# Input and modulation weights laid out in 4 KB runs, small vectors merged, and one engine's order written out in the first stage of a two-layer attention and convolution backbone

## The chip, the cores and the metric

The kernel runs on one core of a Trainium2 chip. The metric is device microseconds of one execution, the median of three runs. A profiled execution of the same kernel gives the trace: the span from its first to its last instruction, and the engines PE (matrix products), DVE (vector), ACT (scalar and activation), POOL (general) and SP, whose queue issues nearly all DMA transfers. "PEld" is PE's loading of weights, and a "q" behind an engine's name marks its queue issuing a DMA.

## The reference, cut to what matters

```
# latent x: 1024 tokens of 1024 channels, context ctx: 256 tokens, conditioning vectors c and c_ctx; all float32
# layer 0 is windowed attention, layer 1 a Conformer convolution
shift, scale, gate     = split(silu(c)    @ ada_w[0] + ada_b[0], 3)
shift_c, scale_c, ...  = split(silu(c_ctx) @ ada_w[0] + ada_b[0], 3)
h_lat = rmsnorm(x, norm_g[0])   * (1 + scale)   + shift
h_ctx = rmsnorm(ctx, norm_g[0]) * (1 + scale_c) + shift_c
proj  = h_lat @ attn_w_in        # 16 query heads, 4 key and 4 value heads, 16 gate heads, 128 columns each
...                              # windowed softmax with a sink and all context keys, times silu(z), @ attn_w_out
x     = x + gate * y
...                              # layer 1: modulation by ada_w[1], ada_b[1]; @ conv_w_in + conv_b_in; GLU; depthwise
...                              # convolution of 31 taps; LayerNorm; silu; times silu(z); @ conv_w_out; x + gate * y
out   = rmsnorm(x, final_g)
```

## The kernel before

Every float32 product is made of three fp32r products: a matrix is split into a rounded part (`hh`, `whi`) and a remainder (`hl`, `wlo`), and `mm3` issues three matmuls of 128x512. A weight column block is 1024x128. `WStream` loads one ("wraw", 512 KB), ACT copies it to `whi`, DVE or POOL subtracts to `wlo`.

The data lives in 45 pages of 128x1024 float32, handed out in the order in which they came free. A DMA into a page waits until the page's last reader is done, and everything behind it in SP's queue waits too. A scheduler orders the instructions of each engine, except of engines named in `pin(...)`: those keep the order of the program.

The first stage computes the modulation and the first three column blocks (k, q and v of the first head). It works on eight channel tiles `kt` of 128 channels. For each tile:

- `ada_load(kt)` has loaded 1 MB of `ada_w`: the shift and scale columns of this tile, in two pages `araw`.
- `ada_mm(kt)` multiplies them with silu(c) and silu(c_ctx) (`c32`): sixteen small matmuls. They leave four partial sums, at partitions 0, 32, 64 and 96, which DVE adds to a row tile `R` ("arow"). Partition 4 of it holds `ada_b`, and the other partitions are zeroed ahead by POOL.
- `ada_cols(kt)` multiplies the rows by a 0/1 matrix `sel`, which adds the parts and turns them into columns; DVE writes them into `mods[kt]` ("mod").
- `turn(xs0, kt)` transposes four 128x128 pieces of the normalised first 512 tokens into `psg`.
- `x_tile` makes `hh` (ACT), `hf` (DVE) and `hl` (DVE) of it, and `x_mm` adds the tile's three matmuls to each of three accumulators in `pss`.

Around it stand `sums` (the squares of a row tile on ACT, into "junk", with their sum in "ssx"), `rstd_of` and `scale_rows`, which normalise the rows ("x_page<-x_page,r"). They run for the first 512 tokens `xs0` at the start, for the second 512, `xs1`, while the tiles go by, and for the context `cx` at the end. `spin` issues matmuls on zeros at the very start. After the eight tiles the second 512 tokens follow in the same manner (`turn(xs1, ...)`, `x_tile(..., half 1)`), then the context; then head by head the rest of the projection and the attention, with four more `wraw` loads issued at once between the two. The convolution layer and the final normalisation end the program.

Of the kernel before, what the change touches and what calls it, by code (L numbers as in the profile page):

```python
# [14 lines left out]
P = 128  # L15
# [79 lines left out]
def backbone_kernel(  # L95
    ctx_stack: ExitStack,
    tc: tile.TileContext,
    x, c, ctx, c_ctx, ada_w, ada_b, norm_g, attn_w_in, attn_sink, attn_w_out,
    conv_w_in, conv_b_in, conv_dw_w, conv_dw_b, conv_ln_g, conv_ln_b, conv_w_out, final_g,
    k_cos, k_sin, k_mask, k_ident, k_sel,  # L100
# [61 lines left out]
    ident = ctile([P, P], F32, "ident")  # L162
    vt = ctile([P, P], F32, "vt")
    sel = vt[:, 112:114]
    sink = ctile([P, 2 * NH], F32, "sink")[:, 0:NH]
# [7 lines left out]
    crow = crow_pg[0:32, 0:P]  # L173
# [28 lines left out]
    class WStream:  # L202
# [52 lines left out]
    W = attn_w_in[0]  # L255

    def wcol(c0):
        return W[:, c0:c0 + P]
# [39 lines left out]

    def load_vecs():
        v = pg.alloc(F32, [2 * P], "vecs")  # L300
# [1430 lines left out]
```

## Time and profile before

| | |
|---|---|
| median of three runs | 1729.6 us (1728.45 to 1730.24) |
| the profiled execution's own time | 1727.67 us |
| its span | 1725.9 us, 24046 instructions |
| granted TensorE clock over the span | 0.993 |
| busy share of the span | PE 98%, PEld 83%, DVE 64%, POOL 52%, ACT 51% |
| moved by DMA | 242.46 MB in 203533 packets; 134999 of them under 2 KB |

A row of the timeline reads: start and duration in microseconds, engine, line, operation, the tiles written and read (out<-in), shape, how many instructions were merged, and in brackets how long the engine stood idle before it and who ended that. Almost all rows have line 89, a helper that records every operation, so the tiles tell the place. A row of the windows reads: the stretch, its length, the busy time of PE, PEld, DVE, ACT and POOL with instruction counts, the granted clock, the DMA share and GB/s.

### The profile page before, as it was taken

The numbers are of one execution on the slowest core, as the hardware profiler recorded it, in microseconds if no ns is written. First come the engines' busy times: TensorE is split into PE (matmuls) and PEld (weight loads), VectorE is DVE, ScalarE is ACT, GpSimd is POOL, SyncE is SP. The second block draws the span as 40 slices with busy tenths as digits, with TensorE's granted clock in tenths as the row PEclk, the third lists the DMA queues.
The fourth block names the chain that finished last, engine by engine and source line by source line (L and its number), as shares of the span: only waits on it lengthen the run. The fifth ranks groups of instructions, "written<-read, shape, count | busy, mean of one in ns | idle before, by whom it ended". The sixth has DMA issues, their size and how long they took to land.

```text
span 1725.9 us, 24046 instructions
## 1 busy us (share of the span) xinstructions
PE 1694.5 (98%) x8489; PEld 1425.7 (83%) x8489; DVE 1096.1 (64%) x2090; ACT 873.3 (51%) x1531; POOL 895.4 (52%) x741
## 2 busy tenths in 40 slices
PE   8799999999999999999999999999999999999997
PEld 5588888888888888888888888888888888788886
DVE  4655553555445553555315179999999999967923
ACT  3555553555345444545334355564665565466731
POOL 1145664566636565653101257999998888130400
PEclk9899999999999999999999999999999999999999
DMA  9334443444334543436777723011121202376971
GB/s 284 124 101 142 136 137 84 147 150 149 99 107 147 159 141 88 135 121 205 252 262 245 258 86 110 25 49 37 42 82 38 91 32 80 122 251 246 337 270 49
DMA packets 203533, 242.46 MB, mean 140 GB/s; under 512 B 11807, under 2 KB 134999, under 8 KB 203413
## 3 DMA queue, kind: packets, MB, share of 16 engines
q1 hardware_dynamic: 197012, 230.43, 40.4%
q10 hardware_dynamic: 6400, 10.49, 2.5%
q8 instruction: 67, 1.10, 0.3%
q14 instruction: 54, 0.43, 0.1%
HBM read 188.70 MB, written 41.69 MB: 133 GB/s over the span
## 4 chain that ended last, share of the span: by engine, by line
PE 91%; DMA 3%; DVE 2%; SPq 2%; ACT 1%; issue 1%; POOL 1%; ACTq 0%; DVEq 0%; POOLq 0%
PE psg L89 47%; PE pss L89 23%; PE pso L89 20%; SPq L89 2%; DMA low_page<-in_conv_w_out_dram 1%; DMA rope_half<-rope_half 1%; DMA x_page<-in_x_dram 0%; DMA araw_page<-in_ada_w_dram 0%; POOL rope_half L89 0%; DVE hf_page L89 0%; DMA ozf_page<-ozd 0%; DMA wraw_page<-in_attn_w_in_dram 0%; ACT lhi_half L89 0%; DVE hl_page L89 0%; DVE ptlo L89 0%
## 5 line engine op out<-in xcount | busy, mean ns | idle before, releaser
L89 POOL TENSOR_TENSOR odd_half<-odd_half,prod_half 128x513 f32<-128x513 f32 (+2 forms) x252 | 313.5, 1251 | 23.3 <-ACT prod_half L89 10.0
L89 PE MATMUL psg<-hh_page,whi_page 128*128 128x512 f32 x600 | 235.6, 393 | 0.0
L89 PE MATMUL psg<-hl_page,whi_page 128*128 128x512 f32 x600 | 234.4, 391 | 0.0
L89 PE MATMUL psg<-hh_page,wlo_page 128*128 128x512 f32 x600 | 233.9, 390 | 0.0
L89 POOL TENSOR_TENSOR wlo_page<-wraw_page,whi_page 128x512 fp32r<-128x512 f32 (+1 forms) x106 | 177.5, 1690 | 96.4 <-ACT whi_page L89 71.1
L89 ACT ACTIVATE prod_half<-ubuf,dww 128x513 f32<-128x513 f32 (+2 forms) x252 | 165.4, 675 | 115.0 <-POOL odd_half L89 111.3
L89 POOL TENSOR_SCALAR p_page<-p_page,sc 128x640 f32<-128x640 f32 (+1 forms) x128 | 99.1, 774 | 223.9 <-DVE sc L89 218.1
L89 PE MATMUL psg<-h2h_page,whi_page 128*128 128x512 f32 x464 | 181.9, 392 | 0.0
L89 PE MATMUL psg<-h2h_page,wlo_page 128*128 128x512 f32 x464 | 180.6, 389 | 0.0
L89 PE MATMUL psg<-h2l_page,whi_page 128*128 128x512 f32 x464 | 180.6, 389 | 0.0
L89 DVE SCALAR_TENSOR_TENSOR pss<-ubuf,dww,pss 128x512 f32<-128x512 f32 (+3 forms) x270 | 172.7, 672 | 0.1
L89 DVE SCALAR_TENSOR_TENSOR pss<-ubuf,wsum,pss 128x512 f32<-128x512 f32 (+3 forms) x270 | 172.0, 672 | 0.2
L89 DVE TENSOR_TENSOR ptlo<-pss,pthi 128x640 fp32r<-128x640 f32 (+1 forms) x144 | 103.5, 719 | 85.7 <-ACT pthi L89 84.6
L89 ACT ACTIVATE pthi<-pss 128x640 fp32r<-128x640 f32 (+1 forms) x144 | 88.7, 616 | 107.9 <-PE pss L89 98.1
L89 ACT ACTIVATE p_page<-p_page,sc 128x641 f32<-128x641 f32 (+1 forms) x128 | 102.6, 802 | 75.0 <-DVE sc L89 71.3
L89 PEld LDWEIGHTS psg<-hh_page,wlo_page 128*128 128x128 f32 x600 | 112.7, 188 | 24.4
L89 PEld LDWEIGHTS psg<-hh_page,whi_page 128*128 128x128 f32 x600 | 112.8, 188 | 19.4
L89 PEld LDWEIGHTS psg<-hl_page,whi_page 128*128 128x128 f32 x600 | 112.8, 188 | 18.4
L89 ACT ACTIVATE whi_page<-wraw_page 128x1024 fp32r<-128x1024 f32 x88 | 92.6, 1052 | 60.0 <-PE psg L89 19.7
L89 PE MATMUL pso<-h2h_page,whi_page 128*128 128x512 f32 x304 | 118.3, 389 | 0.0
L89 PE MATMUL pso<-h2l_page,whi_page 128*128 128x512 f32 x304 | 118.3, 389 | 0.0
L89 PE MATMUL pso<-h2h_page,wlo_page 128*128 128x512 f32 x304 | 118.3, 389 | 0.0
(247 smaller groups left out, 4019.5 us busy)
## 6 DMA issues: line engine op xcount, KB each, us to landing
wraw_page<-in_conv_w_in_dram SPq DMA_DIRECT2D x48, 512.0 KB
wraw_page<-in_attn_w_in_dram SPq DMA_DIRECT2D x40, 512.0 KB
wol_page<-wolA SPq DMA_DIRECT2D x32, 512.0 KB
wo_page<-in_attn_w_out_dram SPq DMA_DIRECT2D x32, 512.0 KB
wo_page<-in_conv_w_out_dram SPq DMA_DIRECT2D x32, 512.0 KB
wol_page<-wolC SPq DMA_DIRECT2D x32, 512.0 KB
rope_half<-rope_half ACTq DMA_DIRECT2D x80, 128.0 KB
araw_page<-in_ada_w_dram SPq DMA_DIRECT2D x32, 256.0 KB
```

The costliest lines, as they stand in the source:

```text
L89: r = f(*a, **k)
```

## The change

The host hands the weights over in another layout: each 1024x128 column block of `attn_w_in` and `conv_w_in`, and each half tile of the modulation weight of layer 0, is one contiguous block in which a partition's 1024 values stand in one run of 4 KB. Before, such a load read runs of 512 bytes. Each `araw` page is now one DMA instead of two.

The small vectors come in two loads: `k_rows` (c, c_ctx, norm_g and the shift and scale part of `ada_b[0]`, 48 rows) at the start, and `k_vecs` (128 rows), now behind the loads of `xs1` and `cx`. The 0/1 matrix `sel` rides in the load of the identity. The `ada_b` part no longer stands in the row tile: it is transposed with c at the start into columns `bcol` (the scale half plus 1), and the two DVE instructions that write `mods[kt]` add it. So the eight loads of `ada_b` and POOL's zeroing of `arow` go, and DVE's add into `arow` becomes a copy.

In the first stage ACT stays in program order to the end of the tile loop, where before it was released after tile 1. The squares of `xs1` stand two tiles apart in the loop, one of the four on DVE. The normalisation of `xs1` no longer uses POOL. `turn` of the next tile stands ahead of the tile's first `x_mm`.

```diff
     crow_pg = hp.alloc(F32, None, "crow")
...
-    SY.dma_start(out=crow[0:8], in_=c.rearrange("o (r p) -> (o r) p", p=P))
-    SY.dma_start(out=crow[8:16], in_=c_ctx.rearrange("(r p) -> r p", p=P))
-    SY.dma_start(out=ident, in_=k_ident)
-    SY.dma_start(out=crow[16:32], in_=norm_g.rearrange("l (r p) -> (l r) p", p=P))
+    crow = crow_pg[0:48, 0:P]
+    SY.dma_start(out=crow, in_=k_rows)
+    SY.dma_start(out=idsel, in_=k_ident)
...
-            SY.dma_start(out=r, in_=self.srcs[i].rearrange("(k p) n -> p k n", p=P))
+            SY.dma_start(out=r, in_=self.srcs[i])
...
         if kt % 2 == 0:
-            R[kt // 2] = r = hp.alloc(F32, None, "arow")
-            G.memset(r[:, 0:512], 0.0)
-            for j in range(2):
-                SY.dma_start(out=r[4:5, 0:512].rearrange("p (t j n) -> p t j n", t=2, j=2)[:, :, j],
-                             in_=ada_b[0:1, j * D + kt * P:j * D + kt * P + 2 * P].rearrange("o (t n) -> o t n", t=2))
-        araw[kt] = [pg.alloc(F32, [4, 2, P], "araw") for _ in range(2)]
+            R[kt // 2] = hp.alloc(F32, None, "arow")
+        araw[kt] = [pg.alloc(F32, [4, 256], "araw") for _ in range(2)]
         for i in range(2):
-            for j in range(2):
-                SY.dma_start(out=araw[kt][i][:, :, j],
-                             in_=ada_w[0, i * 512:i * 512 + 512, j * D + kt * P:j * D + kt * P + P]
-                             .rearrange("(k p) n -> p k n", p=P))
+            SY.dma_start(out=araw[kt][i], in_=k_ada[kt, i])
...
+    bcol = ctile([P, 16], F32, "bcol")
+    V.tensor_copy(bcol[:, 0:8], tp[:, 32:40])
+    V.tensor_scalar(out=bcol[:, 8:16], in0=tp[:, 40:48], scalar1=1.0, scalar2=None, op0=ALU.add)
...
-    vec_pg = load_vecs()
     xs1 = load_rows(x[0, 512:1024], 4)
     cx = load_rows(ctx[0], 2)
+    vec_pg = pg.alloc(F32, [P], "vecs")
+    SY.dma_start(out=vec_pg, in_=k_vecs)
...
-        r = R[kt // 2][:, kt % 2 * 256:kt % 2 * 256 + 256]
-        tt(V, r, o, r, ALU.add)
+        V.tensor_copy(R[kt // 2][:, kt % 2 * 256:kt % 2 * 256 + 256], o)
...
-    x_tile(tps[0], 0, 0, V)
-    wsA.split()
+    wsA.split(lambda: x_tile(tps[0], 0, 0, V))
...
     x_tile(tps[1], 1, 0, V)
-    pin("PV")
     spin(6)
...
+    ss1 = small([P, 4], name="ssx4", bufs=2)
     for kt in range(1, KT):
         nx = kt + 1
         if nx < KT:
             ada_mm(nx)
+            tp = turn(xs0, nx, ps_g)
         x_mm(kt, 0, acc0, (0,))
...
         if nx < KT:
-            tp = turn(xs0, nx, ps_g)
             ada_cols(nx)
             x_tile(tp, nx, 0, V)
...
-        if kt == 4:
-            ss1 = sums(xs1, (A, A, A, A))
+        for i, eng in {4: ((0, A),), 5: ((1, A), (2, A), (3, V))}.get(kt, ()):
+            square(xs1[i], ss1[:, i:i + 1], eng)
...
-            normalise(xs1, ss1, (G, V, A, V))
+            normalise(xs1, ss1, (V, V, A, A))
             ssc = sums(cx, (A, A))
     x_tile(turn(xs1, 1, ps_g), 1, 1, V)
+    pin("PV")
...
+def _columns(w):
+    return w.reshape(KT, P, -1, P).transpose(2, 1, 0, 3)
```

Three places show what moves on the engines. The first is ACT after the normalisation of `xs0`; `mod0` to `mod7` name the channel tile, and the last number of a name only tells buffers apart. Before:

```order
L89 ACTIVATE x_page_4_95<-x_page_4_95,r24_11_262 128x1024
L89 ACTIVATE hh_page_37_293<-psg_14_283,mod0_204 128x512
L89 ACTIVATE whi_page_40_299<-wraw_page_8_111 128x1024
L89 ACTIVATE whi_page_45_337<-wraw_page_11_119 128x1024
L89 ACTIVATE whi_page_47_341<-wraw_page_12_121 128x1024
L89 ACTIVATE hh_page_42_325<-psg_15_288,mod1_205 128x512
L89 ACTIVATE hh_page_49_371<-psg_19_361,mod2_206 128x512
```

The same place on ACT now:

```order
L89 ACTIVATE x_page_4_92<-x_page_4_92,r24_11_229 128x1024
L89 ACTIVATE whi_page_37_260<-wraw_page_8_103 128x1024
L89 ACTIVATE hh_page_39_263<-psg_14_250,mod0_171 128x512
L89 ACTIVATE hh_page_42_292<-psg_15_255,mod1_172 128x512
L89 ACTIVATE whi_page_45_304<-wraw_page_11_109 128x1024
L89 ACTIVATE whi_page_47_308<-wraw_page_12_111 128x1024
L89 ACTIVATE hh_page_49_339<-psg_20_323,mod2_173 128x512
```

The first weight copy moved ahead of tile 0, and the second and third moved behind tile 1.

The second place is ACT at the end of the tile loop. "junk" are the squares; `x_page_26` to `x_page_29` are the four row tiles of `xs1`, and 30 and 31 those of `cx`. Before:

```order
L89 ACTIVATE junk_page_61_492,ssx4_30_491<-x_page_26_183 128x1024
L89 ACTIVATE hh_page_58_479<-psg_28_469,mod5_209 128x512
L89 ACTIVATE junk_page_62_494,ssx4_30_491<-x_page_27_184 128x1024
L89 ACTIVATE junk_page_63_496,ssx4_30_491<-x_page_28_185 128x1024
L89 ACTIVATE junk_page_64_498,ssx4_30_491<-x_page_29_186 128x1024
L89 ACTIVATE hh_page_65_523<-psg_32_513,mod6_210 128x512
L89 ACTIVATE junk_page_73_591,ssx2_42_590<-x_page_30_191 128x1024
L89 ACTIVATE junk_page_74_593,ssx2_42_590<-x_page_31_192 128x1024
L89 ACTIVATE hh_page_68_558<-psg_35_548,mod7_211 128x512
L89 ACTIVATE sq4_38_576<-ms4_37_574 128x4
L89 ACTIVATE x_page_28_185<-x_page_28_185,r24_41_584 128x1024
L89 ACTIVATE hh_page_37_293<-psg_45_604,mod0_204 128x512
```

The same place on ACT now, where `x_page_25` to `x_page_28` are `xs1`, and 29 and 30 are `cx`:

```order
L89 ACTIVATE hh_page_58_447<-psg_29_434,mod5_176 128x512
L89 ACTIVATE junk_page_61_459,ssx4_18_312<-x_page_25_148 128x1024
L89 ACTIVATE hh_page_62_484<-psg_32_471,mod6_177 128x512
L89 ACTIVATE junk_page_65_496,ssx4_18_312<-x_page_26_149 128x1024
L89 ACTIVATE junk_page_66_498,ssx4_18_312<-x_page_27_150 128x1024
L89 ACTIVATE hh_page_68_525<-psg_35_512,mod7_178 128x512
L89 ACTIVATE sq4_38_543<-ms4_37_541 128x4
L89 ACTIVATE x_page_27_150<-x_page_27_150,r24_41_551 128x1024
L89 ACTIVATE x_page_28_151<-x_page_28_151,r24_41_551 128x1024
L89 ACTIVATE junk_page_73_558,ssx2_42_557<-x_page_29_156 128x1024
L89 ACTIVATE junk_page_74_560,ssx2_42_557<-x_page_30_157 128x1024
L89 ACTIVATE hh_page_39_263<-psg_44_569,mod0_171 128x512
```

The first square of `xs1` moved behind the `hh` of tile 5, and the next two behind that of tile 6. The two squares of `cx` moved from ahead of tile 7 to ahead of the first tile of the second half.

The third place is DVE between the `hl` of tile 6 and that of tile 7. Before:

```order
L89 TENSOR_TENSOR hl_page_66_524<-hf_page_67_525,hh_page_65_523 128x512
L89 TENSOR_TENSOR arow_half_6_160<-pso_34_535,arow_half_6_160 128x256
L89 COPY mod7_211<-pso_36_553 128x2
L89 TENSOR_SCALAR mod7_211<-pso_36_553,vt_70 128x2
L89 TENSOR_SCALAR hf_page_70_560<-psg_35_548,mod7_211 128x512
L89 TENSOR_TENSOR hl_page_69_559<-hf_page_70_560,hh_page_68_558 128x512
```

The same place on DVE now ("ISA junk" is the fourth square with its sum, read out by the row behind it):

```order
L89 TENSOR_TENSOR hl_page_63_485<-hf_page_64_486,hh_page_62_484 128x512
L89 ISA junk_page_67_500,ssx4_18_312<-x_page_28_151 128x1024
L89 ISA ssx4_18_312 128x1
L89 COPY arow_half_6_139<-pso_34_502 128x256
L89 TENSOR_SCALAR mod7_178<-pso_36_520,bcol_136 128x2
L89 TENSOR_SCALAR mod7_178<-pso_36_520,bcol_136,vt_70 128x2
L89 TENSOR_SCALAR hf_page_70_527<-psg_35_512,mod7_178 128x512
L89 TENSOR_TENSOR hl_page_69_526<-hf_page_70_527,hh_page_68_525 128x512
```

A square now stands ahead of the copy of the modulation rows of tile 7. Behind the first stage the order of the engines is the same but for two DVE instructions that trade places and two loads (the mask and the cosines) that swap on SP.

More of the change, by code (lines that the diff above doesn't have):

```diff
@@ L313, in load_rows @@
         return ts
-    SY.dma_start(out=sel, in_=k_sel)
     zer_pg = hp.alloc(F32, None, "zer")
@@ L360, in backbone_kernel, with square @@
     hp.free(zer_pg)
+    def square(t, ss, eng):
+        junk = pg.alloc(F32, [1024], "junk")
+        if eng is A:
+            act(junk, t, AF.Square, accum_out=ss)
+        else:
+            V.tensor_tensor_reduce(out=junk, in0=t, in1=t, scale=1.0, scalar=0.0, op0=ALU.mult, op1=ALU.add,
+                                   accum_out=ss)
+        pg.free(junk)
     def sums(ts, engs):
@@ L365, in sums @@
         for i, eng in enumerate(engs):
-            junk = pg.alloc(F32, [1024], "junk")
-            if eng is A:
-                act(junk, ts[i], AF.Square, accum_out=ss[:, i:i + 1])
-            else:
-                V.tensor_tensor_reduce(out=junk, in0=ts[i], in1=ts[i], scale=1.0, scalar=0.0, op0=ALU.mult, op1=ALU.add,
-                                       accum_out=ss[:, i:i + 1])
-            pg.free(junk)
+            square(ts[i], ss[:, i:i + 1], eng)
         return ss
@@ L1202, in backbone_kernel @@
     boff = {"a": 0, "gl": 16, "z": 32}
-    wsB = WStream(hp=True, lo_eng=lambda i: V if i % 3 == 0 and i > 3 else G, srcs=[W1[:, off[k] + j * P:off[k] + (j + 1) * P] for k, j in border])
+    wsB = WStream(hp=True, lo_eng=lambda i: V if i % 3 == 0 and i > 3 else G, srcs=[k_wconv[off[k] // P + j] for k, j in border])
     zsd = dr.tile([NJ, P, T], F32, tag="zsd", name="zsd")
```

64 lines of the change are left out of this document (27 added, 37 removed).

## The prediction

> **What bounds the kernel now.** I read the page first, then the busy time by stretches, to see in which stage PE is not the limit.
>
> ```profile
> span 1725.9 us, 24046 instructions
> PE 1694.5 (98%) x8489; PEld 1425.7 (83%) x8489; DVE 1096.1 (64%) x2090; ACT 873.3 (51%) x1531; POOL 895.4 (52%) x741
> ...
> 0.00:100.00 100.00, 84.35 (x490) 61.66 (x491) 54.89 (x111) 47.49 (x83) 14.37 (x19) 0.93 0.64 200
> 100.00:1600.00 1500.00, 1493.62 (x7488) 1267.81 (x7487) 980.09 (x1849) 771.35 (x1356) 859.46 (x709) 1.00 0.40 130
> ```
>
> PE is idle 15.65 us in the first 100 us and 6.38 us in the next 1500. So a change to loads and to the first stage can pay only in those first 100 us, and what comes behind moves as a block. Next come the longest of PE's waits there, and the timeline around it.
>
> ```profile
> PE pss L89 <- ACT hh_page L89: 3.6, 1, 3.6
> ...
> 38.44 1.07 PE L89 MATMUL pso<-araw_page,c_page 128*32 128x256 f32 x16
> 42.37 1.99 SPq L89 DMA_DIRECT2D x_page<-in_x_dram  x4
> 42.77 1.07 PE L89 MATMUL pso<-araw_page,c_page 128*32 128x256 f32 x16
> 45.57 1.06 ACT L89 ACTIVATE junk_page<-x_page 128x1024 f32<-128x1024 f32 x1 [7.36 <-DMA x_page<-in_x_dram]
> 46.53 0.19 ACT L89 ACTIVATION_READ_ACCUMULATOR junk_page<-x_page 128x1 f32 x1
> 46.63 0.76 ACT L89 ACTIVATE hh_page<-psg,mod 128x512 fp32r<-128x512 f32 x1
> 47.44 0.80 PE L89 MATMUL pss<-hh_page,whi_page 128*128 128x512 f32 x1 [3.60 <-ACT hh_page L89]
> 54.17 1.07 PE L89 MATMUL pso<-araw_page,c_page 128*32 128x256 f32 x16
> ```
>
> The rows with 16 small matmuls are `ada_mm`, one to a tile, and so the clock of the loop: 4.33 us from tile 5 to tile 6, then 11.40 to tile 7. Between them the scheduler had put the first square of `xs1` ahead of the `hh` of tile 5 on ACT. SP issues `xs1` only at 42.37, its first tile lands at 45.57, and ACT stands 7.36 us with the tile's `hh` behind that square. PE then stands 3.60 us, and its clock falls.
>
> ```profile
> 48.00:54.00 6.00, 5.23 (x17) 4.08 (x16) 2.35 (x6) 4.98 (x9) 0.00 (x0) 0.52 0.85 340
> 64.00:67.40 3.40, 3.24 (x10) 2.33 (x9) 1.50 (x2) 2.27 (x4) 0.00 (x0) 0.51 0.18 41
> ```
>
> At a clock of 0.52 six microseconds do three microseconds' work; that is in the 11.40. The second stretch follows the wait for POOL's share of normalising `xs1`, and costs up to 3.40 x 0.49 = 1.7 us.
>
> **The start (term A).** SP issues five small loads ahead of `xs0`; two remain.
>
> ```profile
> 0.74 0.40 SPq L89 DMA_DIRECT2D crow_half<-in_c_dram  x1
> 2.87 1.85 SPq L89 DMA_DIRECT2D x_page<-in_x_dram  x4
> 6.05 0.20 ACT L89 ACTIVATE warm<-cs 128x1 f32<-128x1 f32 x1
> 6.67 1.06 ACT L89 ACTIVATE junk_page<-x_page 128x1024 f32<-128x1024 f32 x1 [0.42 <-DMA x_page<-in_x_dram]
> 22.23 0.76 ACT L89 ACTIVATE hh_page<-psg,mod 128x512 fp32r<-128x512 f32 x1
> 24.49 2.35 DVE L89 TENSOR_TENSOR wlo_page<-wraw_page,whi_page 128x1024 fp32r<-128x1024 f32 x2
> 27.23 0.61 PE L89 MATMUL pso<-vt,arow_half 128*128 128x2 f32 x4
> ```
>
> Five take 2.13 us, so three fewer let `xs0` start 1.28 us earlier. But ACT is free for the first square only at 6.25, so 0.4 of it counts, perhaps 0.1 more where the table load before it moves too: -0.5. The second `hh`, at 22.23 behind two weight copies, now stands ahead of them and gains 0.9. These copies and DVE's two `wlo` (2.35) move behind it and still end last ahead of the column matmuls at 27.23; those gain what the chain gains, 0.5 to 0.9, and if the earlier data carried all through, 1.28 and more. I take A = -0.8, within -0.5 and -1.9.
>
> **The loop (term B).** Now the square stands behind the `hh` of tile 5. The question is whether the data are there. The packet rates, for a stretch of 512-byte runs and one in which `xs1` and `cx` come in 4 KB runs:
>
> ```profile
> DMA packets 10301, 5.14 MB, mean 342 GB/s; under 512 B 273, under 2 KB 10301, under 8 KB 10301
> ...
> DMA packets 284, 1.03 MB, mean 413 GB/s; under 512 B 32, under 2 KB 32, under 8 KB 284
> ```
>
> Ahead of `xs1` lie 8.39 MB of `araw` and three `wraw` of 0.52 MB, 9.96 MB. At 413 GB/s they take 24.1 us, at 342 they take 29.1. The first tile of `xs0` lands at 6.67, the last three tiles later (0.52 MB in 1.27 us each), at 10.5; 29.1 more is 39.6, and the 45.57 at which the first tile of `xs1` lands shows that the end was slower still. Now the last tile of `xs0` lands at 9.2, the last `araw` 24.1 later at 33.3, and the first tile of `xs1` at 34.6, 11 us earlier. ACT wants it near 41. The wait goes, and with it the half clock: 11.40 becomes 4.33, -7.07. Should the loads gain nothing but the 1.28, the tile would land at 44.3, and the square, one tile later in the order, would still hold up only the `hh` of tile 6, by some 0.7.
>
> [...]
>
> `turn` ahead of the first `x_mm` gives `hl` half a microsecond more time. Where PE waited for `hl` inside a regular tile it was 0.2:
>
> ```profile
> 39.84 0.19 PEld L89 LDWEIGHTS pss<-hl_page,whi_page 128*128 128x128 f32 x1 [0.21 <-DVE hl_page L89]
> ```
>
> I take -0.3 for the five tiles, within 0 and -0.8. `ada_mm` of tile 7 then comes 8.2 us earlier (0.8 + 7.07 + 0.3), at 46.0.
>
> **New waits (terms C and D).** DVE now takes a square of 1024 columns between `hl` of tile 6 and the copy of the modulation rows of tile 7. Behind it wait that copy, the column matmuls, `hh`, `hf` and `hl` of tile 7, and PE. No row shows this square; the nearest is `wlo` of the same shape, 2.35 for two, so 1.2, and with its read-out 1.3. PE's own work between covers some: four transposes and three matmuls.
>
> ```profile
> L89 PE MATMUL psg<-hh_page,whi_page 128*128 128x512 f32 x600 | 235.6, 393 | 0.0
> 58.99 0.69 DVE L89 TENSOR_TENSOR hl_page<-hf_page,hh_page 128x512 fp32r<-128x512 f32 x1
> 59.74 0.49 PE L89 MATMUL pss<-hl_page,whi_page 128*128 128x512 f32 x1 [1.07 <-DVE hl_page L89]
> ```
>
> Transposes need nothing of DVE, but the three matmuls start only when `hl` of tile 6 is there, so what hides is about one of them and the overlap, 0.5 by the 393 ns. C = +0.8, within 0 and +1.3. The wait of 1.07 for `hl` of tile 7 stays as it is.
>
> Next is the normalisation of `xs1` and the first tile of the second half.
>
> ```profile
> 61.04 1.15 ACT L89 ACTIVATE x_page<-x_page,r 128x1024 f32<-128x1024 f32 x1 [1.04 <-DVE r L89]
> 61.04 2.28 DVE L89 TENSOR_SCALAR x_page<-x_page,r 128x1024 f32<-128x1024 f32 x2
> 61.16 1.61 POOL L89 TENSOR_SCALAR x_page<-x_page,r 128x1024 f32<-128x1024 f32 x1 [45.23 <-DVE r L89]
> 62.84 0.88 PE L89 MATMUL psg<-ident,x_page 128*128 128x128 f32 x4 [2.11 <-POOL x_page L89]
> 63.75 0.78 ACT L89 ACTIVATE hh_page<-psg,mod 128x512 fp32r<-128x512 f32 x1 [1.55 <-PE psg L89]
> 66.26 0.60 ACT L89 ACTIVATE vf_half<-pss 128x512 f32<-128x512 f32 x1 [0.95 <-PE pss L89]
> 66.91 0.75 PE L89 MATMUL pss<-hh_page,whi_page 128*128 128x512 f32 x1 [0.16 <-ACT vf_half L89]
> ```
>
> POOL's 1.61 goes, but the last row tile was ready by DVE at 63.32 and is now ready by ACT after 2 x 1.15, at the same distance from 61.04: nothing gained or lost. But the two squares of `cx` now stand on ACT between this and the `hh` of 63.75. Up to here the gain is 8.2 - 0.8 = 7.4. ACT is done with the rows at 61.04 - 7.4 + 2.3 = 55.94, with the squares (1.06 and 0.19 for the sum, twice) at 58.4, then come `hh` (0.78), the first accumulator's copy and `vf`, which is of the same shape (0.60 each): 60.4. PE's matmuls of the second half, at 66.91 behind `vf`, would have come at 59.5. D = +0.9, within 0 (if these squares fall into waits) and +2.4 (if all of it shows). The removed zeroing on POOL, the copy in place of an add and the merged vectors, which land well ahead of their transpose, lie beside other work; I cost them at nothing, and if the copies cost as much as `mod`'s small ones it is 0.1 a tile.
>
> **Behind the stage (term E).** The four `wraw` issued together before the attention:
>
> ```profile
> 86.70 6.90 SPq L89 DMA_DIRECT2D wraw_page<-in_attn_w_in_dram  x4
> 94.73 1.06 ACT L89 ACTIVATE whi_page<-wraw_page 128x1024 fp32r<-128x1024 f32 x1 [1.57 <-DMA wraw_page<-in_attn_w_in_dram]
> 99.58 0.44 PE L89 MATMUL pso<-ident,vf_half 128*128 128x128 f32 x2 [1.04 <-ACT vf_half L89]
> ```
>
> Issuing takes 1.7 us each in 512-byte runs, and 0.46 each (1.85 for four) in the 4 KB runs of `xs0`. The third, which ACT waits for, lands at least 1.57 us earlier, so ACT's wait goes, and PE's 1.04 behind it: E = -1.0, within 0 and -1.04. All later weight loads shorten too, under a PE that stands 6.38 us in 1500.
>
> The sum: -0.8 - 7.07 - 0.3 + 0.8 + 0.9 - 1.0 = -7.5. From the profiled execution's own 1727.67 this gives 1720.2; that execution lies 1.9 below the median of 1729.6, so the median after is 1722.1.
>
> **The rivals.** First, *the loads gain no speed* (the 4 KB runs are held by something else than their length, so that the layout does not do what it says): 0.7 more on the squares and no E, -5.8, so 1723.8. The 413 GB/s of `xs1` speak against it.
>
> Second, *the new waits cost a clock drop*: the waits for C, for `hl` of tile 7, for the rows and for D lie within 10 us, and one stretch more at half clock (1.7) with C and D near their ends (+2.0) gives -3.8, 1725.8; with two stretches it is 1727.5. For it speaks that 2.11 of idle time was enough ahead of 64, against it that PE waits there anyway. [...]
>
> Third, *the waits are all covered*: C and D at 0, the half clock at 64 gone: -7.5 - 1.7 - 1.7 = -10.9, 1718.7.
>
> Fourth, *slower*: the swap of key and query halves in the attention goes by DMA, and PE's next head hangs on it.
>
> ```profile
> rope_half<-rope_half ACTq DMA_DIRECT2D x80, 128.0 KB
> PE psg L89 <- DVE rope_half L89: 0.2, 1, 0.2
> ```
>
> Such a load has 64 rows of 2 KB, four on each of 16 DMA engines. If each has to let a weight packet by, it now waits for 4 KB (16 x 4096 bytes at 413 GB/s, 0.159 us) instead of 512 bytes (0.024 at 342): 0.54 us a load. Slower by over 0.2%, which is about what a measurement of this kernel can tell from no change (3.5 us), needs 7.5 + 3.5 = 11.0 us, or 21 of the 80 exposed: 1733.1. Against it: PE waited once for that chain behind 100 us, 0.2 us.
>
> **How the numbers follow.** The forecast as summed, with its terms inside their bounds (1719.6 to 1724.6): 0.57. No faster loads 0.10; clock drop 0.12; all covered 0.10; slower 0.07; gain and loss within 0.2% by a mishap of several small waits 0.04. Faster by over 0.2%, below 1726.1: 0.57 + 0.10 + 0.10 and 0.07 of the clock drop, 0.84. Within 0.2%: 0.05 and 0.03, 0.08. Slower: 0.08. The range runs from 1718.0, just under all-covered, to 1727.0, which holds most of the clock drop; outside lie the slower case and the tails.
>
> **What would show it.** `ada_mm` of tile 7 near 46 instead of 54.17, ACT without a wait for `xs1`, clock 1.00 from 20 to 49; a DVE square of 1.2 us ahead of tile 7 with PE waiting under a microsecond; the second half's first matmul near 60.4; no PE wait near 92; `araw` stretches near 413 GB/s. I am wrong if ACT still waits for `xs1`, if PE's idle time in the first 93 us stays above 14, or if PE gains idle time behind 100 us.

## The result, and the profile after

The changed kernel takes 1720.0 us (median of six executions, 1716.93 to 1722.54) where the kernel before took 1729.2 (six executions, 1728.27 to 1730.61). The ratio is 0.9945, with a 95% interval of 0.9932 to 0.9958. The forecast was 1722.1 within 1718.0 and 1727.0. The profiled execution of the changed kernel took 1722.54 us; it is the longest of the six, which matters below.

The page of the changed kernel, and its busy time by stretches (PE is the first number behind the length, the granted clock the third from the end):

```profile
span 1720.8 us, 23982 instructions
PE 1694.0 (98%) x8488; PEld 1424.3 (83%) x8488; DVE 1097.0 (64%) x2094; ACT 872.8 (51%) x1530; POOL 891.3 (52%) x736
```

```profile
0.00:100.00 100.00, 90.81 (x526) 66.95 (x527) 57.95 (x124) 50.83 (x91) 17.58 (x21) 0.93 0.55 205
100.00:1600.00 1500.00, 1491.75 (x7474) 1265.40 (x7473) 983.10 (x1848) 773.47 (x1356) 856.66 (x706) 1.00 0.40 131
20.00:49.00 29.00, 27.41 (x209) 18.85 (x209) 17.33 (x36) 9.68 (x14) 0.00 (x0) 1.00 0.87 344
49.00:62.00 13.00, 10.30 (x36) 6.85 (x35) 7.83 (x20) 7.67 (x12) 0.56 (x1) 0.74 0.10 24
```

PE's busy time over the whole span is the same, 1694 us. It is idle 9.2 us in the first 100 where it was idle 15.65, and 8.25 in the next 1500 where it was 6.38. That rise is one of the three signs of being wrong that the prediction names; the other two stayed away. The clock is full from 20 to 49 us now, but at 0.74 from 49 to 62 a stretch at half clock remains.

The timeline around the tile loop, in order of time: `ada_mm` of the last two tiles, ACT's first square of `xs1`, DVE's square, PE's waits behind it, the first transposes of `xs1`, the first matmul of the second half, and the copy pair near 92 us (two transposes of `vf` on PE) that ends the first stage (99.58 before; below "the end mark"):

```profile
40.73 1.05 ACT L89 ACTIVATE junk_page<-x_page 128x1024 f32<-128x1024 f32 x1
40.89 1.07 PE L89 MATMUL pso<-araw_page,c_page 128*32 128x256 f32 x16
45.01 1.07 PE L89 MATMUL pso<-araw_page,c_page 128*32 128x256 f32 x16
46.38 1.22 DVE L89 CUSTOM_DVE_ANT_0 junk_page<-x_page 128x1024 f32<-128x1024 f32 x1
47.99 0.61 PE L89 MATMUL pso<-ident,arow_half 128*128 128x2 f32 x4 [0.62 <-DVE arow_half L89]
51.54 0.50 PE L89 MATMUL pss<-hl_page,whi_page 128*128 128x512 f32 x1 [1.07 <-DVE hl_page L89]
53.74 1.88 PE L89 MATMUL psg<-ident,x_page 128*128 128x128 f32 x4 [1.36 <-DVE x_page L89]
58.87 0.79 PE L89 MATMUL pss<-hh_page,whi_page 128*128 128x512 f32 x1
92.10 0.44 PE L89 MATMUL pso<-ident,vf_half 128*128 128x128 f32 x2 [0.44 <-ACT vf_half L89]
```

From tile 6 to tile 7 it is now 4.12 us, where it was 11.40. The square has no bracket: ACT doesn't wait for `xs1`. Against the rows of before the stage gains this much at each point:

| | before | after | difference |
|---|---|---|---|
| `ada_mm` of tile 5 | 38.44 | 36.79 | -1.65 |
| of tile 6 | 42.77 | 40.89 | -1.88 |
| of tile 7 | 54.17 | 45.01 | -9.16 |
| first matmul of the second half | 66.91 | 58.87 | -8.04 |
| end mark | 99.58 | 92.10 | -7.48 |
| end of the span | 1725.9 | 1720.8 | -5.1 |

The loads: DMA packets from 8 to 30 us.

```profile
DMA packets 2531, 9.22 MB, mean 419 GB/s; under 512 B 283, under 2 KB 283, under 8 KB 2530
```

### The profile page after: what moved, and what is told of

Its sections match the earlier page's. It is cut to its first block, busy times and chain, and to the rows that moved or that the text cites. A ratio compares the mean times of both kernels' runs of the same rounds, so it can differ in the third digit from the quotient of the medians.

```text
span 1720.8 us, 23982 instructions
## 1 busy us (share of the span) xinstructions
PE 1694.0 (98%) x8488; PEld 1424.3 (83%) x8488; DVE 1097.0 (64%) x2094; ACT 872.8 (51%) x1530; POOL 891.3 (52%) x736
## 4 chain that ended last, share of the span: by engine, by line
PE 89%; DMA 4%; DVE 3%; ACT 2%; issue 1%; POOL 1%; ACTq 0%; SPq 0%; POOLq 0%; DVEq 0%
PE psg L89 46%; PE pss L89 23%; PE pso L89 20%; DMA low_page<-in_conv_w_out_dram 1%; DMA rope_half<-rope_half 1%; POOL rope_half L89 1%; DMA low_page<-in_attn_w_out_dram 0%; DMA wo_page<-in_conv_w_out_dram 0%; DMA x_page<-in_x_dram 0%; DVE rq L89 0%; DVE x_page L89 0%; ACT lhi_half L89 0%; POOL wlo_page L89 0%; DMA ozf_page<-ozd 0%; DVE hf_page L89 0%
```

## The experiments

The kernels e1 to e4, e5 to e8 and e9 to e12 ran as groups, each on one chip beside executions of the kernel before (medians there 1731.33, 1728.63 and 1729.61). "Gain" is the distance to that median. The ratio is not the quotient of the two medians; by it e1 gains 7.4 us, e5 9.3 and e4 13.7. The end mark is that of one profiled execution.

| | median us (n) | gain | ratio, 95% interval | end mark |
|---|---|---|---|---|
| e1 layout alone | 1722.82 (6) | 8.5 | 0.9957, 0.9943 to 0.9970 | 91.93 |
| e2 order alone | 1727.44 (12) | 3.9 | 0.9979, 0.9970 to 0.9988 | 96.68 |
| e3 vectors alone | 1727.11 (12) | 4.2 | 0.9979, 0.9968 to 0.9990 | 94.86 |
| e4 earlier squares | 1716.41 (5) | 14.9 | 0.9921, 0.9909 to 0.9934 | 83.94 |
| e5 the change | 1720.30 (5) | 8.3 | 0.9946, 0.9933 to 0.9959 | 91.10 |
| e6 order and vectors | 1720.60 (6) | 8.0 | 0.9952, 0.9937 to 0.9968 | 90.47 |
| e7 layout and vectors | 1720.69 (6) | 7.9 | 0.9951, 0.9938 to 0.9963 | 92.48 |
| e8 512 bytes behind the first blocks | 1720.97 (6) | 7.7 | 0.9953, 0.9940 to 0.9966 | 90.08 |
| e9 the change | 1720.38 (6) | 9.2 | 0.9944, 0.9932 to 0.9957 | 90.17 |
| e10 fourth square on ACT | 1719.30 (6) | 10.3 | 0.9940, 0.9927 to 0.9952 | 89.61 |
| e11 squares of `cx` later | 1720.06 (6) | 9.6 | 0.9947, 0.9932 to 0.9962 | 94.38 |
| e12 earlier squares | 1715.97 (4) | 13.6 | 0.9920, 0.9906 to 0.9933 | 83.51 |

The times expected for e1 to e4 were set against some 1729 us. On that chip the kernel before took 2 us more, and the medians lie 0.3 to 1.4 us above the stated ranges, e2's in the range of its rival; the gains lie inside what was expected.

### One part alone: e1, e2, e3

e1 is the kernel before with the layout only; the order of compute stays that of before.

```diff
-            SY.dma_start(out=r, in_=self.srcs[i].rearrange("(k p) n -> p k n", p=P))
+            SY.dma_start(out=r, in_=self.srcs[i])
...
-            for j in range(2):
-                SY.dma_start(out=araw[kt][i][:, :, j],
-                             in_=ada_w[0, i * 512:i * 512 + 512, j * D + kt * P:j * D + kt * P + P]
-                             .rearrange("(k p) n -> p k n", p=P))
+            SY.dma_start(out=araw[kt][i].rearrange("p a b c -> p a (b c)"), in_=k_ada[kt, i])
```

> The kernel before with the 4 KB layout alone (araw, attention and convolution input weights); the order of every compute engine, the eight ada_b loads and the small loads stay as before. Theory (the gain is the wait of tile 5 for xs1, whichever part ends it): xs1 is loaded some 8 us earlier, ACT's first square of xs1 no longer waits though it still stands ahead of the hh of tile 5, ada_mm of tile 7 comes near 46 to 47 instead of 54.17, and POOL's wait of 2.11 and the order behind it stay: 1719.5 to 1722.5. Rival (the order is what ends the wait, faster loads only shorten transfers that PE covers): the wait stays, 1727 to 1729.

Its timeline, with the square still ahead of tile 5's `hh`:

```profile
37.43 1.05 ACT L89 ACTIVATE junk_page<-x_page 128x1024 f32<-128x1024 f32 x1
42.08 1.07 PE L89 MATMUL pso<-araw_page,c_page 128*32 128x256 f32 x16
46.47 1.07 PE L89 MATMUL pso<-araw_page,c_page 128*32 128x256 f32 x16
55.29 0.88 PE L89 MATMUL psg<-ident,x_page 128*128 128x128 f32 x4 [2.10 <-POOL x_page L89]
```

The square at 37.43 finds its data, and tile 7 follows tile 6 after 4.39 us. The wait for POOL's share of the normalisation is that of before (2.10). The layout alone brings most of the gain, and within the intervals perhaps all. It changes the length of the runs and, for `araw`, the number of loads; the two were not separated.

e2 is the kernel before with the order only.

```diff
-    x_tile(tps[0], 0, 0, V)
-    wsA.split()
+    wsA.split(lambda: x_tile(tps[0], 0, 0, V))
...
-    pin("PV")
     spin(6)
...
+            tp = turn(xs0, nx, ps_g)
         x_mm(kt, 0, acc0, (0,))
...
-            tp = turn(xs0, nx, ps_g)
...
-        if kt == 4:
-            ss1 = sums(xs1, (A, A, A, A))
+        for i, eng in {4: ((0, A),), 5: ((1, A), (2, A), (3, V))}.get(kt, ()):
+            square(xs1[i], ss1[:, i:i + 1], eng)
...
-            normalise(xs1, ss1, (G, V, A, V))
+            normalise(xs1, ss1, (V, V, A, A))
...
+    pin("PV")
```

> The kernel before with the new order alone (ACT pinned to the end of the tile loop, squares of xs1 later and one on DVE, turn ahead of the first matmuls, normalisation without POOL); every load as before. Theory (the gain is the wait of tile 5, whichever part ends it): the first square still starts at 45.6 with its data, but now holds up the hh of tile 6 by under 1 us and that of tile 7 by about as much, and the new waits on DVE and behind the squares of cx come on top: 1723.5 to 1726. Rival (the loads bound the loop, so another order only moves the wait on to the next tiles): 1727 to 1729, with PE waiting 3 us or more in tiles 6 and 7.

```profile
42.82 1.07 PE L89 MATMUL pso<-araw_page,c_page 128*32 128x256 f32 x16
45.98 1.06 ACT L89 ACTIVATE junk_page<-x_page 128x1024 f32<-128x1024 f32 x1 [3.37 <-DMA x_page<-in_x_dram]
46.96 1.07 PE L89 MATMUL pso<-araw_page,c_page 128*32 128x256 f32 x16
51.04 1.23 DVE L89 CUSTOM_DVE_ANT_0 junk_page<-x_page 128x1024 f32<-128x1024 f32 x1 [1.67 <-DMA x_page<-in_x_dram]
52.66 1.02 PE L89 MATMUL pso<-vt,arow_half 128*128 128x2 f32 x4 [2.50 <-DVE arow_half L89]
```

`xs1` lands as late as before (45.98), and ACT still stands 3.37 us for it, but the `hh` of tile 5 is no longer behind that square and tile 7 comes at 46.96. So the order alone clears tile 5: tile 7 comes 7.2 us earlier. But the late load now holds DVE: its square waits 1.67 us for the fourth row tile, the modulation rows of tile 7 stand behind it, and PE waits 2.50 us for them. From 50 to 60 us the clock is 0.66, and at the end mark 2.9 us are left. The rival, that another order only moves the wait on, is half right.

e3 is the kernel before with the small vectors only.

```diff
-            G.memset(r[:, 0:512], 0.0)
-            for j in range(2):
-                SY.dma_start(out=r[4:5, 0:512].rearrange("p (t j n) -> p t j n", t=2, j=2)[:, :, j],
-                             in_=ada_b[0:1, j * D + kt * P:j * D + kt * P + 2 * P].rearrange("o (t n) -> o t n", t=2))
...
-    vec_pg = load_vecs()
     xs1 = load_rows(x[0, 512:1024], 4)
     cx = load_rows(ctx[0], 2)
+    SY.dma_start(out=vec_pg, in_=k_vecs)
```

> The kernel before with the small vectors alone (two loads, sel with the identity, ada_b through bcol, no zeroing by POOL, a copy in place of the add); weights still in 512-byte runs, order as before but for one square of xs1 that the scheduler puts ahead of the same tile's hh. Theory (the gain is the wait of tile 5): SP is free of 16 small issues, xs1 lands 3 to 5 us earlier and the wait for it shrinks from 7.4 to between 2 and 4, PE's of 3.6 to under 1, with no half clock behind it: 1722 to 1726. Rival (small loads lie beside others, and the start counts only 0.5): 1728 to 1729.

SP's queue before: the first of the vector loads, which go on until `xs1` is issued at 42.37:

```profile
38.09 0.73 SPq L89 DMA_DIRECT2D vecs_page<-in_conv_b_in_dram  x1
```

The same queue in e3, and what ACT and PE then wait for:

```profile
35.88 2.16 SPq L89 DMA_DIRECT2D x_page<-in_x_dram  x4
41.44 1.06 ACT L89 ACTIVATE junk_page<-x_page 128x1024 f32<-128x1024 f32 x1 [3.77 <-DMA x_page<-in_x_dram]
44.55 0.49 PE L89 MATMUL pss<-hh_page,whi_page 128*128 128x512 f32 x1 [1.25 <-ACT hh_page L89]
```

The small loads alone had held SP's queue by 6.5 us ahead of `xs1` (35.88 instead of 42.37): six vector loads from 38.09 on, a pair of `ada_b` loads (1.2 to 1.8 us) ahead of each two tiles, and three loads at the start. `xs1` lands 4.1 us sooner in the old layout, and PE's wait of 3.60 falls to 1.25, with tile 7 at 49.08. The profiled execution, 1722.19 us, was the fastest of the twelve.

### One part left out: e5, e6, e7

e5 is the changed kernel itself, for comparison on one chip.

> The changed kernel unaltered, beside the three below on one chip. Every theory expects 9 to 10 us below the kernel before, as in the first comparison; it is there so that differences of 1 to 3 us between variants are taken on one chip.

It gained 8.3 us by the medians and 9.3 by the ratio.

e6 is the changed kernel with 512-byte runs, so order and vectors without the layout.

```diff
-            SY.dma_start(out=araw[kt][i], in_=k_ada[kt, i])
+            for j in range(2):
+                SY.dma_start(out=araw[kt][i].rearrange("p a (b c) -> p a b c", b=2)[:, :, j],
+                             in_=ada_w[0, i * 512:i * 512 + 512, j * D + kt * P:j * D + kt * P + P]
+                             .rearrange("(k p) n -> p k n", p=P))
```

> The changed kernel with its 4 KB runs taken back to runs of 512 bytes; order of ACT and the two small vectors stay. Theory (the wait of tile 5 has three cures that each suffice): the three ACT waits of before stay gone or under 1.5 us, tile 7's modulation matmuls start near 46 to 47 us, and the time is 5 to 8.5 us below before, that is 1 to 4 us above the changed kernel. Rival (the layout is needed): xs1 lands near 44 us again, ACT waits over 3 us for it, and no more than 4 us are gained over before.

Its timeline and its stretch from 8 to 30 us:

```profile
42.16 1.06 ACT L89 ACTIVATE junk_page<-x_page 128x1024 f32<-128x1024 f32 x1 [2.02 <-DMA x_page<-in_x_dram]
44.36 1.07 PE L89 MATMUL pso<-araw_page,c_page 128*32 128x256 f32 x16
90.47 0.44 PE L89 MATMUL pso<-ident,vf_half 128*128 128x128 f32 x2 [1.03 <-ACT vf_half L89]
8.00:30.00 22.00, 19.72 (x141) 13.10 (x140) 12.41 (x26) 8.87 (x14) 2.69 (x2) 1.00 1.14 345
```

The loads run at 345 GB/s, ACT waits 2.02 us for `xs1`, and this costs nothing, since behind that square stands only the `hh` of tile 6, which is wanted later; tile 7 comes at 44.36. ACT's first wait is over the 1.5 us that the theory allowed, and yet the gain is 8.0 us: the layout isn't needed once the other two parts are there. The 1 to 4 us above the changed kernel that were expected did not come; it is 0.3.

e7 is the changed kernel without the order part (the loop and squares as before, on ACT).

```diff
-    wsA.split(lambda: x_tile(tps[0], 0, 0, V))
+    x_tile(tps[0], 0, 0, V)
+    wsA.split()
...
+    pin("PV")
     spin(6)
...
-            tp = turn(xs0, nx, ps_g)
         x_mm(kt, 0, acc0, (0,))
...
+            tp = turn(xs0, nx, ps_g)
...
-        for i, eng in {4: ((0, A),), 5: ((1, A), (2, A), (3, V))}.get(kt, ()):
-            square(xs1[i], ss1[:, i:i + 1], eng)
+        if kt == 4:
+            ss1 = sums(xs1, (A, A, A, A))
...
-            normalise(xs1, ss1, (V, V, A, A))
+            normalise(xs1, ss1, (G, V, A, V))
...
-    pin("PV")
```

> The changed kernel with the order part taken out: ACT squares as in the kernel before, layout and two small vectors stay. Theory (order adds only its own waits once the loads are early): no ACT wait for xs1, none of the new DVE-square and x-row waits at 46 to 54 us, the marker (the last half-head copy pair of the first stage on PE) near 91 us, and 9 to 11 us below before, level with the changed kernel or up to 1.5 us better. Rival (the order is needed): ACT's squares of tile 5 hold PE again by 2 us or more, and the gain is 7 us or less.

```profile
37.76 1.04 ACT L89 ACTIVATE junk_page<-x_page 128x1024 f32<-128x1024 f32 x1
42.39 1.07 PE L89 MATMUL pso<-araw_page,c_page 128*32 128x256 f32 x16
46.90 1.07 PE L89 MATMUL pso<-araw_page,c_page 128*32 128x256 f32 x16
```

No wait for `xs1` again. A tile takes 4.51 us here and 4.12 in the changed kernel, and tile 7 comes 1.9 us later than there (46.90 against 45.01). At the end mark (92.48; about 91 was expected) it is 0.4 us behind the changed kernel's profile, 1.4 behind e5 and 2.3 behind e9, which are the same kernel at a mean clock of 0.93, 0.95 and 0.97 over the first 100 us; e7 is at 0.97. The times are level, 1720.69 against 1720.30 in e5. So the order part shows a gain in the first stage and none in the time; what takes it back was not shown.

So the wait of tile 5 had three cures. The layout alone removes it. The order alone removes it too, but moves the wait on to tile 7; the vectors alone leave a third of it. In time each of these two alone brings about half, and both together bring all.

### Behind the first stage: e8

The changed kernel with 512-byte runs for all weights that load behind the first three blocks.

```diff
-        chunks.append(src)
+        cols.append(src)
+        chunks.append(k_win[src // P])
...
+    for q in range(3, len(chunks)):
+        chunks[q] = attn_w_in[0][:, cols[q]:cols[q] + P]
```

> The changed kernel with 512-byte runs for all weights that load behind the first three blocks (attention and input weights, convolution weights), 4 KB for the first. Theory (what a page of weights waits for behind the first stage is the page coming free, not its length of run): within 1 us of the changed kernel, and PE's wait near 92 us between 0.4 and 1.0 us. Rival one (the layout's gain at the weights ahead of attention is real): 1 us or more slower, with that wait back at 1.0 us or more. Rival two (4 KB packets hold up the small transfers of the attention stage): 1 to 5 us faster, with the waits behind 100 us shorter.

The four `wraw` issues and the end mark in e8, and then the four issues in the changed kernel, from the timelines:

```profile
77.31 7.09 SPq L89 DMA_DIRECT2D wraw_page<-in_attn_w_in_dram  x4
90.08 0.44 PE L89 MATMUL pso<-ident,vf_half 128*128 128x128 f32 x2 [0.89 <-ACT vf_half L89]
```

```profile
79.79 7.05 SPq L89 DMA_DIRECT2D wraw_page<-in_k_win_dram  x4
```

The last of the four in e8 takes 0.37 us by itself, and four in 4 KB runs spread over 7.05 us, as four in 512-byte runs do (7.09 here, 6.90 before). The spacing isn't the run length: in all three traces SP's queue waits there, 3.4 to 3.7 us for DVE and 2.1 to 2.3 us for PE, that is, for pages to come free. PE's wait at the end mark is 0.89 us against 0.39 in e5, so the layout is worth 0.5 us here. The time is 0.7 above e5, within the spread of either, and smaller packets brought no gain behind 100 us.

### Single terms undone: e9, e10, e11

e9 is the changed kernel again, the control of this group.

> The changed kernel unaltered, beside the three below on one chip: 8 to 10 us below the kernel before, waits of PE at the DVE square (0.6 us) and for the first row tile of xs1 (1.4 us), and a stretch at half clock behind them.

Its timeline where ACT and PE go from the rows of `xs1` to the second half:

```profile
44.98 1.07 PE L89 MATMUL pso<-araw_page,c_page 128*32 128x256 f32 x16
53.72 1.88 PE L89 MATMUL psg<-ident,x_page 128*128 128x128 f32 x4 [1.37 <-DVE x_page L89]
58.85 0.79 PE L89 MATMUL pss<-hh_page,whi_page 128*128 128x512 f32 x1
```

e10 takes the fourth square back to ACT (term C undone).

```diff
-        for i, eng in {4: ((0, A),), 5: ((1, A), (2, A), (3, V))}.get(kt, ()):
+        for i, eng in {4: ((0, A),), 5: ((1, A), (2, A), (3, A))}.get(kt, ()):
```

> The changed kernel with the fourth square of xs1 on ACT, ahead of the hh of tile 7, instead of on DVE (term C undone). Theory (the square on DVE costs the 0.6 us of PE's wait for the modulation rows): that wait goes, but hh of tile 7 now comes behind three squares; with 3.1 us of squares between two tiles of 4.1 us ACT still makes it, or is late by up to 0.7 us. Time within 1 us of the changed kernel. Rival (the choice of DVE saves time): hh of tile 7 comes over 1 us late, and the time is 1 us or more above the changed kernel.

```profile
44.82 1.07 PE L89 MATMUL pso<-araw_page,c_page 128*32 128x256 f32 x16
48.05 0.78 ACT L89 ACTIVATE hh_page<-psg,mod 128x512 fp32r<-128x512 f32 x1 [0.23 <-DVE mod L89]
52.66 0.30 PE L89 MATMUL psg<-ident,x_page 128*128 128x128 f32 x1 [1.37 <-DVE x_page L89]
57.77 0.49 PE L89 MATMUL pss<-hh_page,whi_page 128*128 128x512 f32 x1 [0.49 <-ACT vf_half L89]
```

ACT has done three squares and still waits 0.23 us for the tile. From tile 7 to the first transposes of `xs1` it is 7.84 us instead of 8.74: the square on DVE costs 0.9 there. Part of it is lost again at the second half, where PE, with a shorter stretch at half clock in this run (mean clock 0.87 from 49 to 62 us, 0.74 in e9), is done earlier and waits 0.49 us for `vf`. The median is 1.1 lower, within the spread of either.

e11 puts the two squares of `cx` behind the first two `hh` of the second half (term D undone).

```diff
-            ssc = sums(cx, (A, A))
     x_tile(turn(xs1, 1, ps_g), 1, 1, V)
+    ssc = sums(cx, (A, A))
```

> The changed kernel with the two squares of cx behind the first two hh of the second half instead of ahead of them (term D undone). Theory (the squares cost nothing in the changed kernel because PE stands at half clock there and cannot use an earlier hh): hh comes 2 us sooner, the first matmul of the second half at most 1 us sooner, and the time is level within 1 us. Rival (D costs what was forecast, 0.9 us, or more): the first matmul comes 1 to 2.4 us sooner, and so does the copy pair that marks the end of the stage.

```profile
56.99 1.88 PE L89 MATMUL psg<-ident,x_page 128*128 128x128 f32 x4 [1.36 <-DVE x_page L89]
58.91 0.78 ACT L89 ACTIVATE hh_page<-psg,mod 128x512 fp32r<-128x512 f32 x1 [0.57 <-PE psg L89]
62.12 0.80 PE L89 MATMUL pss<-hh_page,whi_page 128*128 128x512 f32 x1
```

The `hh` comes 1.9 us behind the first transposes instead of 3.3 (57.05 in e9), and the first matmul of the second half stands at the same distance from them, 5.13 us, as in e9. Both run at half clock for a part of it (mean clock 0.81 from 49 to 62 us, 0.74 in e9), so PE isn't done sooner. Later it waits 0.80 us at 69 instead. The squares cost nothing where the change put them, as long as the clock is down there. (This execution stands 3.2 us behind e9 at tile 7 already, 48.22 against 44.98, so its end mark and its time, the longest of its six, say nothing of the squares.)

### An earlier place: e4 and e12

What the changed kernel still loses is the chain from the squares to the rows, behind which PE waits and its clock falls (0.74 from 49 to 62 us). This version (run twice, e12 being the same file) squares `xs1` and `cx` at tiles 3 and 4, takes one root for all six, normalises at tile 5 on POOL and ACT, and issues the first transposes of `xs1` one step sooner.

```diff
+        else:
+            turn_vecs()
+            tp = turn(xs1, 0, ps_g)
         x_mm(kt, 0, acc0, (0,))
...
+            if kt == 5:
+                r1 = rstd_of(ss1, D, 6)
             x_tile(tp, nx, 0, V)
+            if kt == 5:
+                scale_rows(xs1, r1, (G, G, A, A))
+                scale_rows(cx, r1[:, 4:6], (G, G))
...
-        for i, eng in {4: ((0, A),), 5: ((1, A), (2, A), (3, V))}.get(kt, ()):
-            square(xs1[i], ss1[:, i:i + 1], eng)
+        for i in {3: (0, 1, 2), 4: (3, 4, 5)}.get(kt, ()):
+            square((xs1 + cx)[i], ss1[:, i:i + 1], A)
...
-            normalise(xs1, ss1, (V, V, A, A))
-            ssc = sums(cx, (A, A))
...
-        if kt == 0:
-            normalise(cx, ssc, (V, A))
```

> The changed kernel with what is now late moved up: the squares of xs1 and cx on ACT behind tiles 4 and 5 (three each), one reciprocal root for all six row tiles ahead of tile 6, the rows scaled by POOL (four) and ACT (two) during tiles 6 and 7, and the transposes of the second half's first tile ahead of tile 7's matmuls. Theory (what is left in the first stage are the waits for the fourth square, for the rows of xs1, for the squares of cx and for the rows of cx, and the half clock behind them): of the changed kernel's waits 0.62, 1.36 and 1.05 go, the 1.07 for hl of tile 7 is partly filled, and at least one stretch of half clock goes too: 4 to 8 us below the changed kernel, 1712 to 1716. Rival (POOL's scaling slows DVE beside it, and the waits come back in tiles 6 and 7): 1719 to 1722.

> The version with the squares of xs1 and cx at tiles 3 and 4, one normalisation for both and the first transposes of xs1 one tile ahead, again, beside the changed kernel on one chip. Theory (what the changed kernel still loses in its first stage is the waits and the half clock that the late squares make): no half clock between 20 and 100 us, the end marker of the stage 7 to 8 us sooner, and the time 3 to 5 us below the changed kernel. Rival (the first comparison was the luck of the throttle): within 1.5 us of it.

A window of e12 and PE's wait near 1585 us, and then the same of e9:

```profile
20.00:100.00 80.00, 76.27 (x484) 60.08 (x483) 51.07 (x102) 46.41 (x87) 25.24 (x21) 1.00 0.48 171
1585.06 1.13 PE L89 MATMUL pso<-ident,r 128*128 128x128 f32 x8 [2.72 <-DVE r L89]
```

```profile
20.00:100.00 80.00, 74.28 (x453) 56.41 (x453) 51.73 (x103) 42.31 (x79) 15.48 (x14) 0.96 0.47 170
1584.86 1.13 PE L89 MATMUL pso<-ident,r 128*128 128x128 f32 x8 [0.62 <-DVE r L89]
```

The clock is full throughout, PE is busy 2 us more and issues 31 instructions more in the same 80 us. The end mark stands 6.7 us earlier (7 to 8 were expected) and the median is 4.4 us lower than e9's; the four executions lie within 1714.85 and 1717.03, e9's six within 1716.83 and 1721.53. It beats both kernels, with a gain of 13.6 to 14.9 us (13.7 and 13.8 by the ratios). Why the time gains less than the mark is settled in part. Against e9, instruction by instruction, e12's lead shrinks from 6.3 us at 300 to 4.0 at 600 us, by 1.7 at a half-clock stretch from 802 to 805 that e9 doesn't have, and by 2.1 near 1585, where PE waits for `r`: that comes at the same time in both, so another chain than PE's sets the pace there. These two profiled executions end level (1715.2 and 1715.0); e9's is the fastest of its six and e12's the slowest of its four. In e4, the same file as e12, that wait is missing. What takes the lead between 300 and 600 was not found.

## Why the prediction was right, point by point

**Right.** The bound was the wait of tile 5 in a stage of 100 us, and that stage holds the gain. Tile 6 to tile 7 fell from 11.40 to 4.12, -7.28 where B had -7.07; ACT's wait is gone and the clock is full from 20 to 49.

**Term A and the turn, too small.** At tile 5 the gain was 1.65, and 1.88 at tile 6, where A and the turns together made about 1.0. Two rows of the changed kernel show the start: ACT's first square (6.67 before), and the column matmuls that stood at 27.23:

```profile
5.97 1.05 ACT L89 ACTIVATE junk_page<-x_page 128x1024 f32<-128x1024 f32 x1
25.83 0.61 PE L89 MATMUL pso<-ident,arow_half 128*128 128x2 f32 x4 [0.96 <-DVE arow_half L89]
```

A was -1.4 by the second row against the forecast -0.8, inside its bounds. A tile went from 4.33 to 4.10 us (5 to 6), 0.2 instead of the 0.06 that -0.3 over five tiles makes; in e2, with the order alone, it is 4.14 from 42.82 to 46.96 too, so this is the order's. Why the older order took 4.33 was not separated. `ada_mm` of tile 7 so came at 45.01, one microsecond ahead of the 46.0 forecast.

**The loads (the rival that they gain no speed).** The layout did what it says, 419 GB/s against 342. But the step "should the loads gain nothing but the 1.28, the tile would land at 44.3" failed. It counted the small loads at the start and left out those in SP's queue between the `araw` pages and ahead of `xs1`. In e6, at 345 GB/s, ACT had the tile at 42.16, and the gain was 8.0, not 5.8. That the layout decides was the wrong emphasis: it suffices and isn't needed. The runs do differ from 8 to 30 us (345 GB/s in e6, 419 in the changed kernel), but e6 shows that this kernel doesn't need the difference.

**Term C, right in size.** PE waits 0.62 at the DVE square, and e10 makes its whole cost 0.9; the forecast was 0.8.

**Term D, zero while the clock is down.** The forecast was 0.9 for the squares of `cx` ahead of `hh`. e11 shows no difference up to the first matmul of the second half. What the step missed is that PE runs at half clock just there (0.50 from 53.20 to 60.02), so that its own work covers twice as much. So the second rival came half true: the clock did drop (0.74 from 49 to 62, which is 6.8 us at half clock), but where it dropped, PE would otherwise have waited for what stands behind these squares, as the 0.49 us in e10, with half of that half-clock time (0.87 from 49 to 62), show. The third rival, all waits covered, had it right for D and wrong for C.

**Term E, right sign, wrong reason.** PE's wait went from 1.04 to 0.44, so it did not vanish as forecast, and by e8 the layout is worth 0.5 of the 0.6. The price of 1.7 us an issue was wrong: an issue takes 0.37 us, and the four are as far apart in either layout, because the queue waits for the pages.

**Slower by the rope loads.** Not seen. PE's wait for that chain, near 264 us, is 0.28 to 0.65 us in the traces of the changed kernel (0.2 before), and 0.78 in e8 with the smaller packets.

**The total.** The first matmul of the second half came at 58.87, 1.5 us ahead of the 60.4 forecast. A and the turn gave 1.0 of it. From tile 7 to ACT's first normalised row it took 7.89 us (45.01 to 52.90) where it had taken 6.87, so C took 0.2 beyond its 0.8. From that row to the matmul it took 5.97 where it had taken 5.87, so D gave 0.8.

```profile
52.90 2.19 ACT L89 ACTIVATE x_page<-x_page,r 128x1024 f32<-128x1024 f32 x2 [1.10 <-DVE r L89]
```

From the matmul to the end mark the stage lost 0.56 us, where E should have given 1.0. In e9, the same kernel, it gained 1.35 there, and the end mark came 9.41 earlier. The two executions differ by a stretch at half clock, first the changed kernel's profile, then e9's:

```profile
70.30:73.70 3.40, 3.40 (x9) 2.52 (x9) 1.81 (x4) 0.85 (x3) 0.00 (x0) 0.50 0.00 0
```

```profile
70.30:73.70 3.40, 3.40 (x21) 2.88 (x20) 2.03 (x5) 1.89 (x5) 0.00 (x0) 1.00 0.00 0
```

At a clock of 0.50 these 3.40 us cost 1.7. Over the first 100 us the mean clock is 0.93 in before and in this profile, 0.95 in e5 and 0.97 in e9. So the agreement of the measured 7.48 at the end mark with the forecast 7.5 is partly luck. Behind the mark this profile lost 2.4 us more against before, so its 1722.54 lies above the 1720.2 forecast for a profile; the median lies 2.1 us below the 1722.1 forecast for it.

**What comes behind did not move as a block.** The prediction took this for granted, and named idle time behind 100 us as a sign of being wrong. It came, 8.25 us against 6.38. Matched instruction by instruction, this profile stays 7.0 to 7.8 us ahead of before up to 1000 us, and then loses 1.4 and 1.3 us at two waits that the trace of before doesn't have:

```profile
998.13 0.50 PE L89 MATMUL pss<-woh_page,ozh_page 128*128 128x512 f32 x1 [1.07 <-DVE rq L89]
1590.59 1.13 PE L89 MATMUL pso<-ident,r 128*128 128x128 f32 x8 [1.23 <-DVE r L89]
```

The same kernel has both in e5 (1.10 and 1.54 us) and only the second in e9 (0.62), so they differ between executions; why was not found. From the end mark to the end of the span it is 1628.7 us in this profile and 1624.8 in e9, with the same order of work. Of these 3.9 us, 1.6 go to a half-clock stretch near 807 (clock 0.51 from 807.50 to 810.90, 1.00 in e9), 1.4 to the wait near 998, and 0.6 to that near 1590.

## What to carry to other kernels

When an engine waits for a load, list everything that stands ahead of it in the issuing queue, small loads included, before pricing bytes: here small loads held a 2 MB load back by 6.5 us. Several edits that each cure one wait don't add up (8.5, 3.9 and 4.2 us alone, 8 to 9 together), so undo them one by one and look for the next chain, which here paid 4.4 us more. Keep the work that prepares the next stage off the last tiles of this one: squares and normalisation one or two tiles earlier found their cover, where late they made waits and a fall of the clock (mean 0.96 from 20 to 100 us in e9, 1.00 in e12).

## What the runs showed of the hardware that was not expected

In the changed kernel's profile half clock set in at 53.20, inside a wait of 1.36 us and behind waits of 0.62 and 1.07, and lasted to 60.02 (0.50 throughout). In e8, with the same order of work there, it lasted half as long (mean clock 0.87 from 49 to 62 us, where it is 0.74 in the changed kernel's profile). In e12, where PE waits 0.68 and 0.25 us in the same place, there was none (1.00).

Whether the clock falls at a later place differs between executions of one kernel with the same order of work: from 70.30 to 73.70 it is 0.50 in the changed kernel's profile and 1.00 in e9, and from 807.50 to 810.90 it is 0.51 and 1.00. What decides it was not shown. It is part of why six executions of the changed kernel spread over 5.6 us: between these two profiles it goes with 1.9 us from the first matmul of the second half to the end mark, and with 1.6 near 807.

DVE's square with its sum over 128x1024 took 1.22 us and ACT's 1.05, so moving one to DVE saved nothing that ACT didn't have to spare. DVE scaled two row tiles of `xs1` in 2.28 us where POOL scaled one beside it (before, e1), and in 1.42 us where POOL didn't (the changed kernel, e9).
